# Two classical rows ahead of the Strassen chunks of a down projection, with its operand pieces loaded raw and split by ACT, DVE and POOL

## The chip, the cores and the metric

The kernel runs on one core of a Trainium2 chip. The metric is device time in microseconds (us) for one execution, and less is better. The profile is of one execution. Engines are named as there: PE (TensorE), DVE (VectorE), ACT (ScalarE), POOL (GpSimd) and SP (SyncE, which here only issues DMA).

## The reference

One step of a streaming encoder layer over T = 1072 tokens (16 meta, 1024 prompt, 32 decode), model width 1024. A mixing block (convolution heads and attention heads) comes first. The change is in the feed-forward behind it:

```python
h = rmsnorm(x, g)
u = h @ w_up                       # 1024 -> 2 x 2816
gate, up = u[..., :D_FF], u[..., D_FF:]
y = silu(depthwise_causal_conv(concat(gate_past, gate), dw_w, dw_b)) * up
return x + y @ w_down              # 2816 -> 1024, then the final rmsnorm
```

## The kernel before

Everything is fp32 carried as two parts: `hi` (an ACT cast) and `lo` (raw minus hi, on DVE), both made by `hilo`. A product takes three matmuls (hi hi, hi lo, lo hi). The 2816 hidden channels are 22 rows f = 0..21 of 128, and the 1024 outputs are 8 blocks m.

**Up projection.** Rows 0 and 1 are plain matmuls. Rows 2..21 use Strassen's scheme on 2x2 blocks: seven products q, each for two token halves p, 12 matmuls of 264 to 266 columns each (`product`, L1208), so 168 matmuls per f. The weight combinations of the next f are made by `w_forms` on ACT and DVE meanwhile; `gate_done` and `y_done` make row f of y. For f = 2..17 `y_done` stores the seven right-hand operands to DRAM (`yq`, and for q = 1 and 5 already split, `yh`). The rows 0, 1 and 18..21 are stored whole (`yd`).

**Down projection.** Rows 2..17 form two chunks c = 0, 1 of eight rows. For each chunk there are four Strassen steps mp = 0..3 (two output blocks each), 168 matmuls a step, over 14 operand pieces (q, p) of 128 x 1056 values. They live in the tiles `bh`, `bl` (q = 1..4) and `th`, `tl` (q = 5..7), where the up projection's own operands were. A piece can only be written when PE has finished its last product from the old content: `f_load` is called behind each product of f = 21 (for c = 0) and of step c = 0, mp = 3 (for c = 1). Ten of the 14 pieces come raw through a stage (`early`: row tiles and `rbt`; `late`: `rbt`, `rbg`, shown in the trace as `rb` and `rbg`), four come split from `yh` by POOL's queue. Results go from PSUM to the residual tiles `X` (`x` in the trace), by ACT copies or DVE adds. In c = 0 the old residual `xd` is added by POOL's accumulating DMAs behind each step. The six rows 0, 1, 18..21 stay classical: 18 matmuls for each of 8 blocks m in the end loop over `ENDS` (400, 400 and 256 columns), which also does the final norm (`final`).

PE's order is the order of the code (`manual_schedule`). In the end loop ACT's and DVE's orders are the code's too; elsewhere a scheduler orders them, and each engine then runs its list in order, waits included. PSUM tiles `mm` come from a pool of six.

Of the kernel before, what the change touches and what calls it, by code (L numbers as in the profile page):

```python
# [17 lines left out]
P = 128  # L18
# [74 lines left out]
DN = 264  # L93
FORD = (*range(2, 10, 2), *range(3, 10, 2), *range(10, 18, 2), *range(11, 18, 2), 0, 1, 18, 19, 20, 21)
# [62 lines left out]
def body(nc, tc, cp, wp, xp, dp, io):  # L157
# [922 lines left out]
    yh = dp.tile([2, P, 2, 2, 2, 4, DN], F32, tag="yh", name="yh")  # L1080
# [49 lines left out]
    with tc.tile_pool(name="psB", bufs=1, space=PSUM, reuse_waits="tile") as pf:  # L1130
# [5 lines left out]
        raws3 = [xf[1][:, i * 1024:i * 1024 + 1024] for i in range(3)]  # L1136
# [27 lines left out]
        def w_forms(key, src, raws):  # L1164
            w = ups[key] = Up()
            g, u, s = raws
            A, B = slice(0, 512), slice(512, 1024)
            nc.sync.dma_start(g, src[0])
            nc.sync.dma_start(u, src[1])
            yield  # L1170
            hg, lg, h12, l12, h34, l34, a22 = (free.pop(0) for _ in range(7))
            tt_ = nc.vector.tensor_tensor
            nc.scalar.copy(hg, g)
            tt_(out=s[:, A], in0=u[:, A], in1=u[:, B], op=ALU.add)
            tt_(out=s[:, B], in0=s[:, A], in1=g[:, A], op=ALU.subtract)
# [12 lines left out]
            used = (h12, l12, hg, lg, h34, l34, a22)
            free.extend(z for z in used if key != ("d", 0, 0) or not any(z is r for r in rawr))
# [77 lines left out]
        def y_done(f):  # L1267
# [38 lines left out]
        SEQ_ = (1, 5, 6, 2, 7, 3, 4)  # L1306
        FIRST, COPY = (1, 5, 2), (1, 5, 6, 4)
# [17 lines left out]
        def strassen(key, steps, dst, ns, fresh=True):  # L1325
            banks = {}
            for q, p in steps:
# [3 lines left out]
                product(banks[k], q, p, key, ns[p], q in FIRST)  # L1331
                for lo_, hi_, z in dst(*OUT[q], p):
                    if fresh and q in COPY:
# [75 lines left out]
        def rows(z, n):  # L1409
            z = z.rearrange("p a b c -> p (a b c)") if len(z.shape) == 4 else flat(z) if len(z.shape) == 3 else z  # L1410
            w = T - H0 if n == KD else ny
            return [z[:, i * w:i * w + ny] for i in range(n)]

        trow = [(h, l) for p in range(2) for h, l in zip(rows(THI[p], 3), rows(TLO[p], 3))]
        yrow = [trow[i] for i in (0, 3, 1, 4, 2, 5)]
        yf = (0, 1, 18, 19, 20, 21)
        early = [rows1[0][:, 0:ny], rows1[1][:, 0:ny], rbt[:, 0:ny]]
        early += early[:1] + 3 * early[1:]
        late = [rbt[:, 0:ny], rbg[:, 0:ny]]
        nst = [-1]  # L1420

        def stage(st):
            nst[0] += 1
            return st[nst[0] % len(st)]

        def f_load(c, q, p):
            if q in (1, 5):
                for j, z in enumerate(form(q, p, DN)):
                    nc.gpsimd.dma_start(z, yh[c, :, q // 5, j, p].bitcast(F32R))
                return  # L1430
            raw = stage(late if c else early)
            nc.sync.dma_start(raw, yq[c, :, q - 1, p].rearrange("p a b -> p (a b)"))
            hilo(*form(q, p, DN), raw.rearrange("p (a b) -> p a b", b=DN))

        def y_load(i):
            raw = stage(late)
            nc.sync.dma_start(raw, yd[yf[i]][:, NMETA:T])
            hilo(*yrow[i], raw)

        bhf, blf = flat(BH), flat(BL)  # L1440
# [9 lines left out]
        def d_src(m, f0, f1):  # L1450
            return d.wdn[m, :, f0:f1, :].rearrange("p a b -> p (a b)")

        def d_load(m):
            w = 6 * P
            if m < 4:
                hi, lo = free.pop(0), free.pop(0)
            else:
                hi, lo = (z[:, (m - 4) * 1024:(m - 4) * 1024 + 1024] for z in (bhf, blf))
            raw = fraw()
            nc.sync.dma_start(raw[:, :w], d_src(m, 16, 22))  # L1460
            hilo(hi[:, :w], lo[:, :w], raw[:, :w])
            return kv(hi[:, :w]), kv(lo[:, :w])

        def d_mm(ps, w, t0, n):
            at = t0 - NMETA
            mm3(ps, range(6), lambda k: w[0][:, k, :], lambda k: w[1][:, k, :],
                lambda k: yrow[k][0][:, at:at + n], lambda k: yrow[k][1][:, at:at + n])

        pairs = [(q, p) for q in SEQ_ for p in range(2)]
        apart = [(q, p) for p in (1, 0) for q in SEQ_]  # L1470

        def dn_forms(c, mp):
            if (c, mp) == (0, 0):
# [15 lines left out]

        for f in range(2, NF - 1):  # L1490
            run(up_strassen(f, pairs), w_forms(f + 1, [up_src(f + 1, u) for u in range(2)], raws3))
        run(up_strassen(NF - 1, apart), dn_forms(0, 0), lambda q, p: f_load(0, q, p),
            (1, 3, 5, 9, 10, 11, 12))
        ends = {}

        def last_hook(q, p):
            if p:
                if q in (5, 6, 7):
                    y_load(2 * (q - 5))
                    y_load(2 * (q - 5) + 1)  # L1500
                if q in (6, 2, 3, 4):
                    m = len(ends)
                    ends[m] = d_load(m)

        steps = [(c, mp) for c in range(2) for mp in range(4)]
        for i, (c, mp) in enumerate(steps):
# [153 lines left out]
```

## Time and profile before

| | |
|---|---|
| median of 3 runs | 1095.97 us (1094.5 to 1096.67) |
| the profiled execution | 1095.29 us |
| its span | 1093.5 us (1.79 us around it) |
| PE / DVE / ACT / POOL busy share | 96% / 79% / 46% / 15% |
| mean granted clock of PE | 0.988 |

PE is busy in nearly every slice, so time is lost where PE waits. Stages: mixing to about 352 us, up projection to about 825, down steps to 1009, end loop to 1082, final norm and stores to 1093.5.

### The profile page before, as it was taken

How to read it: one execution, taken by the hardware profiler on the slowest of the kernel's cores; microseconds unless marked ns; L12 is line 12 of the kernel's file. 1: busy time of each engine (PE TensorE's matmuls, PEld its weight loads, DVE VectorE, ACT ScalarE, POOL GpSimd, SP SyncE). 2: the span in 40 equal slices, each digit the busy share in tenths (PEclk: the TensorE clock that was granted, in tenths of full speed). 3: DMA queues.
4: the chain of work that ended last, by engine and by line, in shares of the span. 5: the costliest groups of instructions: out<-in, count | busy, mean ns of one | idle time of the engine just before them, and what ended most of it. 6: DMA issues, size and time to landing. Idle time of an engine off the chain costs nothing.

```text
span 1093.5 us, 19782 instructions
## 1 busy us (share of the span) xinstructions
PE 1050.1 (96%) x7741; PEld 1019.4 (93%) x7741; DVE 860.3 (79%) x1559; ACT 499.8 (46%) x1077; POOL 168.2 (15%) x205
## 2 busy tenths in 40 slices
PE   8999999989999989999999999999998999799996
PEld 7999997758999989999999999999997999799996
DVE  7799999999887797888888879888768447666344
ACT  8532227996766854344344344334335334213321
POOL 1111000012334010010110011010021131000232
PEclk9999998999999999999999999999999999899998
DMA  7344331125853111432432432332287469414113
GB/s 263 80 108 100 82 95 40 39 59 82 158 147 134 41 59 59 139 107 89 122 124 89 127 119 89 112 134 89 85 261 226 127 132 330 143 39 152 45 49 112
DMA packets 73062, 125.46 MB, mean 115 GB/s; under 512 B 11264, under 2 KB 53496, under 8 KB 72968
## 3 DMA queue, kind: packets, MB, share of 16 engines
q1 hardware_dynamic: 56232, 97.44, 27.4%
q0 software_dynamic: 16448, 26.54, 12.8%
q8 instruction: 61, 1.00, 0.4%
q14 instruction: 33, 0.27, 0.1%
q10 hardware_dynamic: 288, 0.22, 0.1%
HBM read 83.23 MB, written 31.83 MB: 105 GB/s over the span
## 4 chain that ended last, share of the span: by engine, by line
PE 55%; DVE 6%; DMA 3%; ACT 3%; issue 2%; POOL 0%; POOLq 0%; DVEq 0%; ACTq 0%; SPq 0%
PE mm L1208 46%; PE mm L241 3%; PE mm L239 3%; PE mm L240 3%; DMA x<-yq 1%; DVE tl L1146 1%; DMA raw<-wdn 1%; DVE bl L1146 1%; ACT hraw L1228 1%; DMA x<-wdn 0%; ACT th L1145 0%; DMA rbg<-yq 0%; DVE x L1336 0%; DVE sl L1146 0%; DMA rb<-yq 0%
## 5 line engine op out<-in xcount | busy, mean ns | idle before, releaser
L365 DVE SCALAR_TENSOR_TENSOR acc<-glu,prm,acc 128x1090 f32<-128x1090 f32 (+3 forms) x180 | 168.0, 968 | 0.4
L1208 PE MATMUL mm<-bh,sl 128*128 128x264 f32 (+1 forms) x752 | 163.0, 286 | 1.8 <-ACT bh L1145 1.3
L1208 PE MATMUL mm<-th,sl 128*128 128x264 f32 (+1 forms) x592 | 144.6, 287 | 2.6 <-ACT gx L1334 1.9
L1208 PEld LDWEIGHTS mm<-bh,sl 128*128 128x128 f32 x752 | 125.9, 190 | 2.3 <-ACT bh L1145 1.6
L1208 PE MATMUL mm<-bl,sl 128*128 128x264 f32 (+1 forms) x376 | 108.2, 288 | 0.9 <-DVE bl L1146 0.9
L1208 PEld LDWEIGHTS mm<-th,sl 128*128 128x128 f32 x592 | 104.1, 189 | 3.4 <-ACT gx L1334 2.1
L239 PE MATMUL mm<-hi,whi 128*128 128x352 f32 (+3 forms) x312 | 104.7, 336 | 0.7 <-ACT hi L274 0.7
L1208 PE MATMUL mm<-bh,whi 128*128 128x264 f32 (+1 forms) x384 | 102.2, 288 | 2.2 <-DVE x L1336 1.2
L240 PE MATMUL mm<-lo,whi 128*128 128x352 f32 (+3 forms) x312 | 102.3, 328 | 1.7 <-DVE lo L275 1.7
L1208 PE MATMUL mm<-bh,wlo 128*128 128x264 f32 (+1 forms) x384 | 101.6, 287 | 0.2 <-DVE x L1336 0.2
L241 PE MATMUL mm<-hi,wlo 128*128 128x352 f32 (+3 forms) x312 | 101.8, 326 | 0.0
L1208 PE MATMUL mm<-tl,sl 128*128 128x264 f32 (+1 forms) x296 | 85.1, 288 | 3.3 <-DVE tl L1146 3.2
L1336 DVE TENSOR_TENSOR x<-x,mm 128x264 f32<-128x264 f32 (+6 forms) x190 | 61.3, 352 | 31.8 <-PE mm L1208 31.1
L1334 ACT COPY x<-mm 128x264 f32<-128x264 f32 (+4 forms) x138 | 43.9, 339 | 80.1 <-PE mm L1208 75.4
L1208 PE MATMUL mm<-th,wlo 128*128 128x264 f32 (+1 forms) x272 | 77.7, 285 | 0.0
L1208 PE MATMUL mm<-th,whi 128*128 128x264 f32 (+1 forms) x272 | 77.6, 285 | 0.0
L1208 PEld LDWEIGHTS mm<-bh,whi 128*128 128x128 f32 x384 | 70.9, 192 | 2.8 <-ACT bh L1145 1.4
L1208 PEld LDWEIGHTS mm<-bl,sl 128*128 128x128 f32 x376 | 71.7, 191 | 1.1 <-DVE bl L1146 1.1
L1208 PEld LDWEIGHTS mm<-bh,wlo 128*128 128x128 f32 x384 | 70.6, 191 | 0.4 <-DVE x L1336 0.4
L240 PEld LDWEIGHTS mm<-lo,whi 128*128 128x128 f32 x312 | 59.2, 190 | 3.4 <-DVE lo L275 3.1
L1208 PE MATMUL mm<-bh,rawr 128*128 128x264 f32 (+1 forms) x272 | 61.5, 286 | 0.0
L239 PEld LDWEIGHTS mm<-hi,whi 128*128 128x128 f32 x312 | 59.1, 189 | 2.2 <-ACT hi L274 1.2
(387 smaller groups left out, 3099.7 us busy)
## 6 DMA issues: line engine op xcount, KB each, us to landing
x<-wup SPq DMA_DIRECT2D x40, 512.0 KB, 4.9
wlo<-raw POOLq DMA_DIRECT2D x16, 512.0 KB, 4.5
yh<-x SPq DMA_DIRECT2D x24, 264.0 KB, 4.9
yq<-x SPq DMA_DIRECT2D x24, 264.0 KB, 2.7
raw<-win SPq DMA_DIRECT2D x12, 512.0 KB, 3.4
raw<-wdn SPq DMA_DIRECT2D x12, 512.0 KB, 4.2
rb<-yq SPq DMA_DIRECT2D x9, 528.0 KB, 4.5
yq<-gx SPq DMA_DIRECT2D x16, 264.0 KB, 5.0
```

Source lines behind the costliest of these rows:

```text
L239: nc.tensor.matmul(ps, whi(k), xhi(k), start=first and i == 0, stop=False)
L240: nc.tensor.matmul(ps, whi(k), xlo(k), start=False, stop=False)
L241: nc.tensor.matmul(ps, wlo(k), xhi(k), start=False, stop=last and i == n - 1)
L365: nc.vector.scalar_tensor_tensor(out=a, in0=e[:, a0 + k:a1 + k], scalar=pcol("cw", p * CW + k), in1=a, op0=ALU.mult, op1=ALU.add)
L1146: nc.vector.tensor_tensor(out=lo, in0=raw, in1=hi.bitcast(F32), op=ALU.subtract)
L1208: nc.tensor.matmul(ps, w[:, j, :], x[:, j, :], start=first and j + i == 0, stop=j == 3 and i == 2, skip_group_check=True)
L1228: nc.scalar.activation(h[:, 2 * i * n + lo_:2 * i * n + hi_], src, AF.Copy, scale=pcol("g2", k))
L1334: nc.scalar.copy(z, banks[k][:, lo_:hi_])
L1336: nc.vector.tensor_tensor(out=z, in0=z, in1=banks[k][:, lo_:hi_], op=ALU.add)
```

## The change

In words:
1. `yh` is gone. All 14 pieces of a chunk are loaded raw from `yq` through a queue of stages (`Feed`: `fill` starts a DMA when a stage is free, `take` splits the piece and gives the stage back). In the fourth Strassen step, behind whose products chunk 1's pieces are loaded, there are three stages (`late`: `rbt`, `gx0`, `rbg`) in place of two. Ten of the 28 low parts are subtracted on POOL.
2. Rows 0 and 1 move from the end loop to a place between f = 21 and the first Strassen step: 24 classical groups of six matmuls (384, 352 and 320 columns), written to `X` by ACT. Chunk 0's pieces are split among them. The end loop has four rows, 12 matmuls per block.
3. All Strassen results are now added by DVE (`fresh=False`), and `xd` is added after steps 0 and 1, as twelve DMAs of POOL's queue.
4. f = 21 runs its products in the order 1, 6, 7, 5, 3, 2, 4, both halves of a product together, instead of all of p = 1 before p = 0. The steps run mp = 3, 2, 1, 0.
5. `w_forms` takes its second weight in two halves of 512 and needs one stage less; `gx0` is free of it.
6. In f = 0 and 1, two steps of the operand preparation `t1s` and the `gate_done(0)` move by a group or two.

```diff
-FORD = (*range(2, 10, 2), *range(3, 10, 2), *range(10, 18, 2), *range(11, 18, 2), 0, 1, 18, 19, 20, 21)
+FORD = (0, 1, *range(2, 10, 2), *range(3, 10, 2), *range(10, 18, 2), *range(11, 18, 2), 18, 19, 20, 21)
...
-        def hilo(hi, lo, raw):
+        def hilo(hi, lo, raw, eng=None):
             nc.scalar.copy(hi, raw)
-            nc.vector.tensor_tensor(out=lo, in0=raw, in1=hi.bitcast(F32), op=ALU.subtract)
+            return (eng or nc.vector).tensor_tensor(out=lo, in0=raw, in1=hi.bitcast(F32), op=ALU.subtract)
...
-            g, u, s = raws
+            g, a, b = raws
...
-            nc.sync.dma_start(g, src[0])
-            nc.sync.dma_start(u, src[1])
+            for z, y in ((g, src[0]), (a, src[1][:, A]), (b, src[1][:, B])):
+                nc.sync.dma_start(z, y)
...
-                for j, z, hi, lo in ((0, b11, form_row(G), form_row(G, 2 * DN)), (1, t1, form_row(Tm, 2 * DN), b11)):
-                    hilo(hi.bitcast(F32R), lo.bitcast(F32R), z)
-                    nc.sync.dma_start(yh[c, :, j, 0, :, i, :], hi)
-                    nc.sync.dma_start(yh[c, :, j, 1, :, i, :], lo)
+                put(1, b11)
+                put(5, t1)
...
-            if i == 2:
+            if i == 1:
                 next(last_rms)
                 gate_done(0)
-            next(t1s)
+            if i % 2:
+                next(t1s)
...
+            def fill(self):
+                while self.jobs and self.stages:
+                    dst, src, view = self.jobs.pop(0)
+                    z = self.stages.pop(0)
+                    raw = view(z)
+                    nc.sync.dma_start(raw, src)
+                    self.ready.append((dst, raw, z))
+
+            def take(self, eng=None, keep=True):
+                dst, raw, z = self.ready.pop(0)
+                self.last = hilo(*dst, raw, eng).ins
+                if keep:
+                    self.stages.append(z)
+                self.fill()
...
-        run(up_strassen(NF - 1, apart), dn_forms(0, 0), lambda q, p: f_load(0, q, p),
-            (1, 3, 5, 9, 10, 11, 12))
+        run(up_strassen(NF - 1, [(q, p) for q in SEQL for p in range(2)]), None, first_hook)
+        TAKES = {0: (None, None), 1: (nc.gpsimd,), 3: (nc.gpsimd,), 4: (None,), 9: (nc.gpsimd,), 12: (None,), 14: (nc.gpsimd,), 17: (None,), 18: (nc.gpsimd,)}
+        for i, (m, b) in enumerate([(m, b) for m in range(KD - 1, -1, -1) for b in (1, 2)] +
+                                   [(m, 0) for m in range(KD - 1, -1, -1)]):
+            for e in TAKES.get(i, ()):
+                feed.take(e, i >= 9)
+                if i == 3:
+                    feed.stages += late
+                    feed.fill()
+            t0, n = YB[b]
+            ps = mmt()[:, :n]
+            d_mm(ps, [z[:, m % 4] for z in wa[m // 4]], arow, t0, n)
+            nc.scalar.copy(X[b][:, m, t0 - OB[b][0]:], ps)
...
-            if mp == 3:
-                hook = last_hook if c else lambda q, p: f_load(1, q, p)
+            if i == 3:
+                feed = Feed([f_job(1, q, p) for q, p in pairs], late)
+                hook = lambda q, p: feed.take(nc.gpsimd if (q, p) in GQ else None)
...
-            run(strassen(("d", c, mp), pairs if i else apart, dn_dst(mp), (DN, DN), c == 0),
-                dn_forms(*steps[i + 1]) if i < 7 else None, hook,
-                *(() if i else ((1, 3, 5, 9, 12, 12, 13),)))
-            if c == 0:
-                for b, (t0, n) in enumerate(YB):
-                    nc.gpsimd.dma_start(X[b][:, 2 * mp:2 * mp + 2, t0 - OB[b][0]:], xd[:, 2 * mp:2 * mp + 2, t0 - H0:t0 - H0 + n],
-                                        accum_op=ALU.add)
+            run(strassen(("d", c, mp), pairs, dn_dst(mp), (DN, DN), False),
+                dn_forms(*STEPS[i + 1]) if i < 7 else None, hook)
+            for z in {0: (0, 1), 1: (3, 2)}.get(i, ()):
+                xd_add(z)
```

How the lists of three engines change. First POOL, at the fourth Strassen step (`bl`, `bh`, `tl`, `th` are operand tiles, `rb` is the stage `rbt`). Before, POOL only issues DMAs there:

```order
L1429 DMA bh_3096<-yh_3103 128x4x264
L1429 DMA tl0_3620<-yh_3103 128x4x264
L1429 DMA th0_3618<-yh_3103 128x4x264
L1429 DMA tl1_3621<-yh_3103 128x1056
L1429 DMA th1_3619<-yh_3103 128x1056
L1515 DMA x0_2250<-xd_3100 128x2x320
L1515 DMA x1_2251<-xd_3100 128x2x384
L1515 DMA x2_2252<-xd_3100 128x2x352
```

After, POOL subtracts four low parts of chunk 1, behind the last adds of `xd`:

```order
L1538 DMA x1_2251<-xd_3100 128x2x384
L1538 DMA x2_2252<-xd_3100 128x2x352
L1145 TENSOR_TENSOR tl1_3620<-rb_75,th1_3618 128x1056
L1145 TENSOR_TENSOR bl_3097<-rb_75,bh_3096 128x4x264
L1145 TENSOR_TENSOR tl1_3620<-rb_75,th1_3618 128x1056
L1145 TENSOR_TENSOR bl_3097<-rb_75,bh_3096 128x4x264
```

All four come through the same stage `rbt`, and no DMA of `yh` is left on that queue.

Second ACT, behind f = 21 (L1335 and L1527 evict PSUM tiles `mm`; L1144 casts a raw stage). Before, at the start of the down steps:

```order
L1145 CAST bh_3096<-x2_2252 128x4x264
L1145 CAST th1_3619<-rb_75 128x1056
L1334 COPY x0_2250<-mm_8608 128x266
L1145 CAST bh_3096<-x2_2252 128x4x264
L1334 COPY x1_2251<-mm_8740 128x176
L1334 COPY x2_2252<-mm_8740 128x88
```

After, at the start of the classical groups:

```order
L1144 CAST th0_3617<-rb_75 128x4x264
L1144 CAST th1_3618<-x1_2251 128x1056
L1335 COPY x0_2250<-mm_8500 128x266
L1335 COPY x0_2250<-mm_8514 128x264
L1144 CAST whi_3635<-raw_8617 128x512
L1527 COPY x1_2251<-mm_8726 128x384
L1144 CAST bh_3096<-x1_2251 128x4x264
L1527 COPY x2_2252<-mm_8736 128x352
L1144 CAST sl_4085<-raw_8617 128x512
L1527 COPY x1_2251<-mm_8748 128x384
L1144 CAST th1_3618<-rb_75 128x1056
L1527 COPY x2_2252<-mm_8761 128x352
```

In both lists casts of staged pieces stand between evictions; after, the evictions are those of classical groups (`mm_8726` is the first), one PSUM tile each.

Third DVE, in the step behind the fourth (L1337 adds a product to `X`, L1145 subtracts a low part, L1176, L1177 and L1182 are weight combinations). After:

```order
L1176 TENSOR_TENSOR raw_9886<-raw_9886 128x512
L1337 TENSOR_TENSOR x2_2252<-x2_2252,mm_9901 128x264
L1145 TENSOR_TENSOR bl_3097<-rbg_3098,bh_3096 128x4x264
L1177 TENSOR_TENSOR raw_9886<-raw_9885,raw_9886 128x512
L1337 TENSOR_TENSOR x0_2250<-x0_2250,mm_9981 128x264
L1145 TENSOR_TENSOR sl_4085<-raw_9885,whi_3635 128x1024
L1145 TENSOR_TENSOR sl_4085<-raw_9886,wlo_3638 128x512
L1337 TENSOR_TENSOR x1_2251<-x1_2251,mm_9995 128x176
L1337 TENSOR_TENSOR x2_2252<-x2_2252,mm_9995 128x88
L1145 TENSOR_TENSOR bl_3097<-gx0_3621,bh_3096 128x4x264
L1337 TENSOR_TENSOR x0_2250<-x0_2250,mm_9887 128x56
```

The adds of products stand behind subtractions of pieces, and the last piece of chunk 1 on DVE (`gx0`) comes well inside the step that uses it.

## Rows read from the trace of the kernel before

**Rows 1.** The head of the page: the span, and each engine's busy time with its share of the span and its count of instructions.

```profile
span 1093.5 us, 19782 instructions
...
PE 1050.1 (96%) x7741; PEld 1019.4 (93%) x7741; DVE 860.3 (79%) x1559; ACT 499.8 (46%) x1077; POOL 168.2 (15%) x205
```

**Rows 2.** Busy time by stretch. Columns: the stretch (us), its length, then for PE, its weight loads, DVE, ACT and POOL the busy us and (x instructions); the granted clock of PE; the busy share of the DMA engines; GB/s.

```profile
400.00:500.00 100.00, 100.00 (x817) 100.00 (x817) 84.24 (x118) 41.50 (x80) 8.70 (x14) 1.00 0.28 94
808.30:853.00 44.70, 35.25 (x254) 32.97 (x253) 32.82 (x44) 21.11 (x35) 7.25 (x9) 0.96 0.84 256
870.00:900.00 30.00, 30.00 (x248) 30.00 (x247) 13.07 (x24) 10.55 (x27) 9.87 (x11) 1.00 0.58 130
925.00:946.00 21.00, 14.22 (x80) 12.76 (x79) 15.05 (x23) 8.01 (x9) 0.00 (x0) 0.84 0.64 175
```

**Rows 3.** What PE waited for between 805 and 855 us: its line, the instruction that let it go, us in total, times, longest.

```profile
PE mm L1208 <- DVE bl L1146: 2.0, 3, 0.9
PE mm L1208 <- ACT gx L1334: 1.9, 1, 1.9
PE mm L1208 <- DVE tl L1146: 1.9, 1, 1.9
PE mm L1208 <- DVE x L1336: 1.4, 2, 1.2
```

**Rows 4.** The same between 922 and 948 us.

```profile
PE mm L1208 <- DVE tl L1146: 3.2, 1, 3.2
PE mm L1208 <- DVE bl L1146: 2.2, 2, 1.2
PE mm L1208 <- ACT bh L1145: 1.3, 1, 1.3
```

**Rows 5.** DMA issues between 895 and 950 us: transfer, queue, count, size, median us from issue to landing.

```profile
rb<-yq SPq DMA_DIRECT2D x4, 528.0 KB, 5.4
rbg<-yq SPq DMA_DIRECT2D x4, 528.0 KB, 4.8
...
bl<-yh POOLq DMA_DIRECT2D x2, 528.0 KB, 9.5
```

**Rows 6.** The same between 800 and 855 us.

```profile
x<-yq SPq DMA_DIRECT2D x6, 528.0 KB, 6.8
rb<-yq SPq DMA_DIRECT2D x5, 528.0 KB, 3.6
```

**Rows 7.** ACT between 800 and 1000 us by line and shape: busy us, mean ns of one, idle before.

```profile
L1145 ACT CAST th<-rb 128x1056 fp32r<-128x1056 f32 x7 | 7.5, 1078 | 5.8 <-PE mm L1208 2.2 <-DMA rb<-yq 2.1 <-DMA rb<-yd 1.4
L1334 ACT COPY x<-mm 128x264 f32<-128x264 f32 x18 | 6.8, 379 | 17.8 <-PE mm L1208 17.6
...
L1145 ACT CAST sl<-raw 128x512 fp32r<-128x512 f32 x7 | 4.4, 623 | 12.9 <-PE mm L1208 8.8 <-DVE raw L1176 3.2 <-DVE raw L1179 0.7
```

**Rows 8.** DVE between 800 and 1000 us, in the same columns.

```profile
L1336 DVE TENSOR_TENSOR x<-x,mm 128x264 f32<-128x264 f32 x38 | 16.0, 424 | 6.2 <-PE mm L1208 5.6 <-issue 0.6
L1146 DVE TENSOR_TENSOR tl<-rb,th 128x1056 fp32r<-128x1056 f32 x7 | 8.8, 1254 | 1.6 <-ACT th L1145 1.6
...
L1176 DVE TENSOR_TENSOR raw<-raw 128x512 f32<-128x512 f32 x6 | 4.1, 684 | 0.0
```

**Rows 9.** POOL over the whole span, in the same columns.

```profile
L1556 POOL TENSOR_TENSOR rb<-rb,gx 128x400 f32<-128x400 f32 x7 | 7.4, 1054 | 16.2 <-ACT gx L1554 16.2
...
L1556 POOL TENSOR_TENSOR rb<-rb,gx 128x256 f32<-128x256 f32 x3 | 2.2, 740 | 6.6 <-ACT gx L1554 6.6
```

**Rows 10.** Four timeline answers set one under the other: start, us, engine and instruction. POOL and then DVE at 1043 us, the same DVE instruction at 1070 us, and DVE and POOL at 350 us.

```profile
1043.58 1.05 POOL L1556 TENSOR_TENSOR rb<-rb,rbg 128x400 f32<-128x400 f32 x1
...
1043.63 1.02 DVE L255 SCALAR_TENSOR_TENSOR stat<-stat 128x4 f32<-128x4 f32 x1 [1.15 <-POOL stat L254]
...
1070.14 0.16 DVE L255 SCALAR_TENSOR_TENSOR stat<-stat 128x4 f32<-128x4 f32 x1 [1.81 <-POOL stat L254]
...
350.39 1.23 DVE L1146 TENSOR_TENSOR wlo<-raw,whi 128x1024 fp32r<-128x1024 f32 x1 [1.13 <-ACT whi L1145]
...
350.90 1.38 POOL L271 TENSOR_TENSOR rb<-rb,acc 128x352 f32<-128x352 f32 x1 [2.58 <-ACT acc L270]
```

**Rows 11.** What PE waited for between 381 and 392 us.

```profile
PE mm L241 <- DVE wlo L1146: 2.1, 1, 2.1
PE mm L239 <- ACT whi L1145: 1.7, 1, 1.7
```

**Rows 12.** Timeline of the last round of the end loop: two PE rows, the ACT row between them, and DVE.

```profile
1067.18 0.95 PE L252 MATMUL R<-ones,rb 128*128 128x1 f32 x8
...
1072.32 1.05 PE L263 MATMUL R<-diag,ones 128*128 128x128 f32 x8
...
1071.44 1.27 ACT L260 ACTIVATE diag<-ident,stat 128x128 f32<-128x128 f32 x4
...
1079.84 0.42 DVE L1553 TENSOR_TENSOR x<-x,mm 128x256 f32<-128x256 f32 x1 [0.38 <-PE mm L241]
...
1081.97 0.42 DVE L1553 TENSOR_TENSOR x<-x,mm 128x256 f32<-128x256 f32 x1 [0.38 <-PE mm L241]
1082.31 1.42 DVE L1530 SCALAR_TENSOR_TENSOR x<-x,prm,R 128x48 f32<-128x48 f32 x4
1083.82 0.16 DVE L253 TENSOR_SCALAR stat<-R 128x2 f32<-128x2 f32 x1
```

More of the change, by code (lines that the diff above doesn't have):

```diff
@@ L1331, in strassen @@
                 product(banks[k], q, p, key, ns[p], q in FIRST)
+                copy = fresh and (OUT[q], p) not in begun
+                begun.add((OUT[q], p))
                 for lo_, hi_, z in dst(*OUT[q], p):
-                    if fresh and q in COPY:
+                    if copy:
                         nc.scalar.copy(z, banks[k][:, lo_:hi_])
@@ L1341, in up_strassen @@
             for q, p in strassen(f, steps, up_dst(f), PNS):
-                if (q, p) == (3, 1) and f < NF - 1:
+                if (q, p) == (3 if f < NF - 1 else 2, 1):
                     gate_done(f)
                 yield q, p
-            if f == NF - 1:
-                gate_done(f)
             y_done(f)
@@ L1388, in body @@
             group(1, u, p, c)
+            if i in (0, 2):
+                next(t1s)
             if i == 3:
@@ L1407, in body @@
         ny = T - NMETA
[L1409 to L1440, printed above, removed]
+        def row(q, p):
+            a = (q - 5) * 4 * PNS[p]
+            return [flat(z[p].rearrange("p a b c -> p (a b) c"))[:, a:a + ny] for z in (THI, TLO)]
+        arow = row(7, 0), row(7, 1)
+        crow = row(5, 0), row(5, 1), row(6, 0), row(6, 1)
+        late = [rbt[:, 0:ny], gx0[:, 0:ny], rbg[:, 0:ny]]
@@ new lines, in body, with __init__ @@
+        class Feed:
+            def __init__(self, jobs, stages):
+                self.jobs, self.stages, self.ready = list(jobs), list(stages), []
+                self.fill()
[11 more added lines that the diff above has]
+                    self.stages.append(z)
+                self.fill()
@@ L1488, in run @@
                 pass
+        GQ = ((5, 1), (2, 0), (7, 1), (4, 0))
+        STEPS = [(c, mp) for c in range(2) for mp in (3, 2, 1, 0)]
         for f in range(2, NF - 1):
-            run(up_strassen(f, pairs), w_forms(f + 1, [up_src(f + 1, u) for u in range(2)], raws3))
-        run(up_strassen(NF - 1, apart), dn_forms(0, 0), lambda q, p: f_load(0, q, p),
-            (1, 3, 5, 9, 10, 11, 12))
-        ends = {}
-        def last_hook(q, p):
[L1497 to L1503, printed above, removed]
@@ L1505, in body @@
[L1505 to L1516 removed]
+            run(up_strassen(f, pairs), w_forms(f + 1, up_srcs(f + 1), raws))
@@ new lines, in body, with first_hook @@
+        first = []
+        def first_hook(q, p):
+            if q == 7:
+                if p == 0:
+                    feeda.take(keep=False)
+                    feeda.jobs.append(w_job(wa[0], 0, 4, 0, 2))
+                    feeda.stages.append(x1a)
+                    feeda.ready.append(feeda.ready.pop(0))
+                    feeda.fill()
+                else:
+                    feeda.take(keep=False)
+                    feeda.take(keep=False)
+            if q == 5 and p:
+                first.append(dn_forms(*STEPS[0]))
+                next(first[0])
+            if q == 3:
+                if p:
+                    feeda.take(keep=False)
+                    feed.stages += [x1b, x2b, rbt]
+                    feed.fill()
+            if q == 2 and p:
+                feeda.take(keep=False)
+                feed.stages += [x1a, x2a]
+                feed.fill()
@@ new lines, in body, with xd_add @@
+        feed = Feed([f_job(0, q, p) for q in (7, 3) for p in range(2)], late)
+        for e in (None, None, None, nc.gpsimd):
+            feed.take(e)
+        mark = feed.last
+        def xd_add(mp):
+            with tc.issue_after(mark):
+                for b, (t0, n) in enumerate(YB):
+                    nc.gpsimd.dma_start(X[b][:, 2 * mp:2 * mp + 2, t0 - OB[b][0]:],
+                                        xd[:, 2 * mp:2 * mp + 2, t0 - H0:t0 - H0 + n], accum_op=ALU.add)
+        wend = []
@@ L1544, in body @@
             for m in range(KD):
-                if not pos and m + 4 < KD:
-                    ends[m + 4] = d_load(m + 4)
                 ps = mmt()[:, :n]
-                d_mm(ps, ends[m], t0, n)
+                d_mm(ps, [z[:, m % 2] for z in wend[m // 2]], crow, t0, n)
                 if m == 0:
```

102 lines of the change are left out of this document (58 added, 44 removed).

## The prediction

> **What bounds the kernel now.** I read the head of the page, the table of stretches, PE's waits in the stretches where PE falls behind, and the DMA landings there. PE is busy 1050.1 of 1093.5 us, DVE 860 [rows 1], so PE sets the time wherever it has its operands. Its own pace is read in the up projection: 817 matmuls in 100 us with nothing missing, 0.1224 us each, 1.47 us for a product of twelve [rows 2]. The count of matmuls in a stretch then tells what PE lost in it, waits and half clock together:
> - **T1**, the change from the up projection to the down steps: 44.70 us held 254 matmuls, worth 254 x 0.1224 = 31.1, so 13.6 us were lost, at a mean granted clock of 0.96 [rows 2].
> - **T2**, the change to chunk 1: 21.00 us held 80, worth 9.8, so 11.2 us were lost, clock 0.84 [rows 2].
>
> Between them PE loses nothing (30.00 of 30.00). A few records can be missing, so each loss may be some tenths smaller. In T1 PE waits for the low and high parts of the new pieces, once 1.9 us for an eviction (`gx`), and for DVE adds [rows 3]; in T2 only for parts of pieces [rows 4]. The reason is the turn of a stage: landing 4.8 to 5.4 us [rows 5], cast 1.08 [rows 7], subtraction 1.25 [rows 8], about 7.3 us. Two stages give a piece per 3.6 us; a product wants one per 1.47. So 24.8 us is all that the change can win at T1 and T2.
>
> **The change, part by part.** I count from the first matmul of a stage, at 1.47 us a product, in the order of the lists.
>
> *T1.* f = 21 takes 14 x 1.47 = 20.6 us. The classical groups do work that the end loop loses, so they cost PE nothing in sum; by the column (18 matmuls of 256 columns take 1081.97 - 1079.84 = 2.13 us, [rows 12]) they take 1.07, 0.98 and 0.89 us for 384, 352 and 320 columns, 23.5 together. In that time chunk 0's pieces can come, and Strassen starts at 44.1. What can still stop PE is ACT's list, where casts that wait for a DMA stand ahead of evictions, with six PSUM tiles as cover (about 6 us). The longest chain is the stage `rbt`: cast of piece (6,0) from 19.1 (behind the first weights' casts), POOL's subtraction, landing of (5,1), cast, POOL, landing of (4,0), cast. A subtraction of 1056 columns on POOL isn't in the trace; 400 columns take 1.054 and 256 take 0.740 [rows 9], 2.18 ns a column, so I estimate 2.48. Sum: 19.1 + 1.08 + 2.48 + 4.8 + 1.08 + 2.48 + 4.8 + 1.08 = 36.9. Behind it the eviction of group 10 (0.4) ends at 37.3, and group 16, which wants that tile, could start at 20.6 + 8 x 2.05 = 37.0. So 0.3 lost there. Two other margins are thin: the low part of the second weight tile of rows 0 and 1 (ready near 20.3, wanted at 20.8), and pieces (7,1) and (3,1), about 2 us ahead of their use. Bounds: 0 with landings of 3.6, about 6 with 6.8 [rows 6]. I take **2.0**, since 4.8 lies nearer the first.
>
> *T2.* Fourth step, t = 0 at its start. Three stages are full, and the pieces are needed from 20.6 on. Stage `rbt` again is the slow one, since POOL empties it four times: its first piece is split by DVE at 5.9 (the next weights land near 2.5, 4.8 behind an issue at -2.3; two casts 0.62 and 1.08 [rows 7], two adds, the subtraction 1.25), then four turns of 4.8 + 1.08 + 2.48 = 8.36 bring the low part of (4,0) at 39.3. PE wants it 26 products in, at 38.2: 1.1 lost. DVE is the second limit. In two steps it has 28 adds (half of them whole, 0.424; half in two parts, about 0.57), 13.9; twenty weight instructions (eighteen of 512 columns at 0.684, two of 1024, about twice that), 15.0; ten subtractions, 12.5 [rows 8]: 41.4 busy, but an instruction starts about 0.08 before the last one ends (1082.31 against 1081.97 + 0.42, [rows 12]), so some 35.6 of the 41.2 us. It fits, but adds wait behind subtractions that wait for casts that wait for DMA: by my count the adds of (7,0) and (7,1) in the fourth step and of (6,0) and (7,0) in the fifth come between 0.7 us early and 1 us late. I take **2.5** in all. Bounds: 0 with 3.6, 5 with 5.4, 10 with 6.8 a landing.
>
> *End loop.* Its groups shrink by a third. In the last 256-column round two groups lie between PE's sums (L252, 1067.18) and its spread of the factor (L263, 1072.32), which needs ACT's four `diag` tiles (1071.44 to 1072.71) [rows 12]. With groups of 1.42 PE is there 1.42 earlier and that chain isn't: 0.9 lost. Then DVE has an add and four scalings per group, 0.34 + 1.42 = 1.76 (or 1.7 with overlap), where PE now takes 1.42; over the last groups it falls behind by 0.9, and the last sums wait for the last add. Before, DVE waited for PE there. Together **+1.8**, bounds 0 and 4.
>
> *T0.* Rows 0 and 1: PE waits 1.7 and 2.1 us for the split of a weight tile [rows 11]. Two preparation steps leave the lists ahead of that split. The second wait stays if its subtraction stays where it is; **-1.0**, bounds 0 and -3.
>
> *At nothing.* `w_forms` has one DVE instruction more for the same columns, and even rows lose two splits: DVE is 84% busy in the up projection and PE 100% [rows 2]. If that cover were gone, 0.684 for each of 20 rows would be 14 us. The adds that move from ACT to DVE, eight a step, put 8 x 0.42 to 0.57 = 4 us on a DVE that was busy 13.07 of 30 us [rows 2]. The `xd` DMAs are first read two steps after their issue; even a POOL transfer of 9.5 us [rows 5] is hidden by 20.6.
>
> **Sum**, against the profiled execution's 1095.3, 0.7 under the median: 1095.3 - 24.8 + 2.0 + 2.5 + 1.8 - 1.0 = 1075.8, so **1076**.
>
> **The rivals.**
>
> *Landings stay long.* The `rbt` chain has two landings in T1 and four in T2. At 6.8 us, T1's median before, each adds 2.0: +12, **1088**. For it: T1 moves some 14 pieces in 40 us now as then. Against: most of the 256 GB/s of T1 [rows 2] went with POOL's split loads, which are gone; `rb` landed in 3.6.
>
> *POOL and DVE get in each other's way.* A DVE instruction of 128x4 that takes 0.16 us took 1.02 while POOL subtracted for 1.05; elsewhere DVE took its 1.23 for 1024 columns while POOL stretched to 1.38 for 352 [rows 10]. So one can hold up the other. If each of POOL's four subtractions at T2 holds DVE for its whole 2.48, DVE has 35.6 + 9.9 = 45.5 of 41.2 us, 4.3 too much; and where DVE goes first, POOL's chain grows by up to 4 x 1.25 = 5. That is +9: **1085**. The Trainium skill says this (SBUF — State Buffer, "SBUF: two separate sides"): GpSimd and a DVE instruction with two SBUF inputs take one pair of ports as an exclusive lock for a whole instruction. The 1.02 agrees; by that rule the sum would be the 1085 just given. Adds read PSUM on one side and would escape it, and four such meetings must each fall on a thin margin, so I hold it less likely.
>
> *Slower than before.* ACT and DVE run their lists in order, so a late landing stops evictions and adds that have nothing to do with the piece. The place is `rbt`'s chain: six landings, 4.5 us lost already at 4.8. The gain of 24.0 (24.8 + 1.0 - 1.8) is gone when 6 e + 4.5 = 24.0, at e = 3.3, that is from 8.1 us a landing. POOL's loads took 9.5 [rows 5]; at that, 6 x 4.7 = 28 more, **1104**. Against: SP's own loads of the same size took 4.8 to 6.8 in the same crowd.
>
> *It doesn't do what it says.* The new weight order makes each of the 20 rows of the up projection a microsecond longer, DVE's 84% being the average over 20 us of which the first part may be full. That is +20: **1096**. Against: PE had no idle there at that load [rows 2], and the work per row doesn't grow.
>
> **How the numbers follow.** Forecast 0.58 (own range 1070 to 1081), long landings 0.19, ports 0.11, slower 0.09, no change 0.03. Under 0.2% (2.2 us) a measurement of this kernel can't be told from no change. The first three are faster: 0.88. The range starts at 1067 (all three remaining losses at nothing and T0 at 3: 1095.3 - 24.8 - 3 = 1067.5) and reaches to 1090, past the long landings; outside lie the last two cases and little else.
>
> **What would show it.** In the new profile: T1 and T2 with over 95% of the matmuls that the pace gives, no half clock there; POOL's 128x1056 subtraction near 2.5 us; SP's `yq` landings near 4.8; waits of PE, if any, at (4,0) of the fifth step and at the third quarter of the classical groups; PE waiting about 0.9 us at L263 in the last round. I am wrong if POOL's subtractions take much longer, if adds (`x`) become PE's main wait in steps four and five, or if the up projection has fewer than 817 in 100 us.

## The result and the profile after

The changed kernel takes 1083.85 us (median; 1083.37 to 1084.88), the kernel before 1095.24 us beside it: ratio 0.9899, 95% interval 0.988 to 0.9919. It is faster by 11.4 us where 19.3 were forecast (1095.3 to 1076). The profiled execution took 1084.88 us, 1.8 of it outside the span.

The head of the page after, against [rows 1]: PE is busy 3 us less, DVE 14 us more.

```profile
span 1083.1 us, 19942 instructions
...
PE 1046.9 (97%) x7741; PEld 1016.4 (94%) x7741; DVE 874.4 (81%) x1616; ACT 499.5 (46%) x1072; POOL 180.7 (17%) x199
```

Busy time by stretch, in the columns of [rows 2]: the up projection, the classical groups, two stretches of the first two Strassen steps, and T2.

```profile
400.00:500.00 100.00, 100.00 (x817) 100.00 (x816) 83.88 (x123) 41.05 (x82) 11.34 (x14) 1.00 0.27 86
...
820.80:850.00 29.20, 25.05 (x147) 23.03 (x146) 24.16 (x23) 18.58 (x36) 12.76 (x7) 1.00 0.57 186
...
850.00:875.70 25.70, 25.70 (x212) 25.70 (x211) 17.35 (x34) 9.38 (x13) 15.85 (x11) 1.00 0.83 215
...
870.00:900.00 30.00, 30.00 (x247) 29.89 (x246) 18.22 (x46) 5.31 (x8) 7.64 (x7) 1.00 0.96 192
921.90:957.00 35.10, 31.77 (x256) 31.19 (x255) 32.48 (x57) 18.07 (x21) 10.71 (x4) 1.00 0.75 232
```

The up projection keeps its 817 matmuls, and the half clock of T1 and T2 is gone (0.96 and 0.84 before, 1.00 now). But the classical groups, 23.5 us of work, take 29.2: 5.7 lost. In T2, 256 matmuls are worth 256 x 0.1224 = 31.3 of 35.1 us: 3.8 lost. What PE waited for, in the columns of [rows 3]: first between 820 and 850 us, then between 921 and 957.

```profile
PE mm L239 <- ACT x L1527: 4.0, 5, 1.2
```

```profile
PE mm L1209 <- DVE x L1337: 3.1, 2, 2.1
PE mm L1209 <- ACT th L1144: 0.2, 1, 0.2
```

PE hardly waits for a piece any more (0.2 us for `th`), as it did in [rows 3, 4]. It waits for PSUM tiles: in the classical groups for ACT's evictions, in T2 for DVE's adds. The timeline shows what stood ahead of these. POOL's subtractions, four of the ten (start, us):

```profile
823.02 2.92 POOL L1145 TENSOR_TENSOR tl<-x,th 128x1056 fp32r<-128x1056 f32 x1
...
829.76 3.36 POOL L1145 TENSOR_TENSOR tl<-rb,th 128x1056 fp32r<-128x1056 f32 x1 [0.49 <-ACT th L1144]
...
923.80 2.86 POOL L1145 TENSOR_TENSOR tl<-rb,th 128x1056 fp32r<-128x1056 f32 x1 [29.35 <-ACT th L1144]
933.08 2.48 POOL L1145 TENSOR_TENSOR bl<-rb,bh 128x1056 fp32r<-128x1056 f32 x1 [6.42 <-ACT bh L1144]
```

DVE beside them:

```profile
823.52 3.54 DVE L1256 TENSOR_TENSOR gx<-gx,rbg 128x1060 f32<-128x1060 f32 x1
...
830.70 3.53 DVE L1262 SCALAR_TENSOR_TENSOR x<-gx,prm,x 128x1058 f32<-128x1058 f32 x1
...
835.97 1.30 DVE L1262 SCALAR_TENSOR_TENSOR x<-gx,prm,x 128x1058 f32<-128x1058 f32 x1
...
924.91 2.83 DVE L1145 TENSOR_TENSOR sl<-raw,wlo 128x1024 fp32r<-128x1024 f32 x1
...
934.22 2.46 DVE L1145 TENSOR_TENSOR bl<-gx,bh 128x1056 fp32r<-128x1056 f32 x1 [0.44 <-ACT bh L1144]
```

The same L1262 takes 1.30 us with POOL idle and 3.53 with POOL subtracting. Each of the four long rows ends 1.1 us behind the end of a POOL row (823.52 + 3.54 = 827.06 against 823.02 + 2.92 = 825.94, and so on): it has waited for POOL and then done its own 1.2 to 1.3 us. ACT, in the classical groups:

```profile
835.47 0.62 ACT L1144 CAST sl<-raw 128x512 fp32r<-128x512 f32 x1 [2.95 <-DVE raw L1185]
...
837.30 1.09 ACT L1265 ACTIVATE x<-x 128x1058 f32<-128x1058 f32 x1 [0.84 <-DVE x L1262]
...
848.48 1.75 ACT L1527 COPY x<-mm 128x320 f32<-128x320 f32 x5 [1.57 <-DMA yd<-x]
```

So DVE's stretched gate chain of row 21 (L1256, L1262) delays a weight combination (L1185), and ACT's cast of it and the evictions behind that cast come late; then ACT's silu (L1265), and at the end the store of that row (`yd`), which the last evictions overwrite. PE waits behind each of these. The next load of the stage `rbg` and the store were issued at 839.7 and 842.3 us; in the first kernel of experiment 4, where this chain isn't stretched, they were issued at 835.3 and 837.2.

### The profile page after: what moved, and what is told of

Its sections match the earlier page's. It is cut to its first block, busy times and chain, and to the rows that moved or that the text cites. A ratio compares the mean times of both kernels' runs of the same rounds, so it can differ in the third digit from the quotient of the medians.

```text
span 1083.1 us, 19942 instructions
## 1 busy us (share of the span) xinstructions
PE 1046.9 (97%) x7741; PEld 1016.4 (94%) x7741; DVE 874.4 (81%) x1616; ACT 499.5 (46%) x1072; POOL 180.7 (17%) x199
## 4 chain that ended last, share of the span: by engine, by line
PE 55%; DVE 6%; DMA 3%; ACT 3%; issue 2%; POOL 1%; POOLq 0%; DVEq 0%; SPq 0%; ACTq 0%
PE mm L1209 49%; PE mm L241 2%; PE mm L239 2%; PE mm L240 2%; DMA raw<-wdn 1%; DVE bl L1145 1%; DMA gx<-yq 1%; DVE tl L1145 1%; DVE x L1262 1%; ACT hraw L1229 1%; DVE sl L1145 1%; DMA yd<-x 1%; DVE x L1582 1%; DVE gx L1256 0%; DVE wlo L1145 0%
## 5 line engine op out<-in xcount | busy, mean ns | idle before, releaser
L1209 PE MATMUL mm<-bh,sl 128*128 128x264 f32 (+1 forms) x912 | 214.7, 285 | 1.0 <-DVE x L1337 1.0
L1209 PEld LDWEIGHTS mm<-bh,sl 128*128 128x128 f32 x912 | 157.6, 189 | 1.2 <-DVE x L1337 1.2
L1209 PE MATMUL mm<-th,rawr 128*128 128x266 f32 (+1 forms) x640 | 121.3, 285 | 0.0
L1337 DVE TENSOR_TENSOR x<-x,mm 128x264 f32<-128x264 f32 (+7 forms) x238 | 75.8, 346 | 47.9 <-PE mm L1209 47.8
L1209 PEld LDWEIGHTS mm<-th,rawr 128*128 128x128 f32 x640 | 101.2, 189 | 0.0
L1209 PE MATMUL mm<-th,sl 128*128 128x264 f32 (+1 forms) x352 | 93.1, 285 | 0.2 <-ACT th L1144 0.2
L1209 PE MATMUL mm<-tl,rawr 128*128 128x266 f32 (+1 forms) x320 | 91.4, 286 | 0.0
L1209 PE MATMUL mm<-bl,whi 128*128 128x264 f32 (+1 forms) x272 | 77.4, 285 | 0.0
L1144 ACT CAST sl<-x 128x512 fp32r<-128x512 f32 (+1 forms) x41 | 29.7, 726 | 76.0 <-PE mm L1209 40.8
L1209 PEld LDWEIGHTS mm<-th,sl 128*128 128x128 f32 x352 | 64.2, 189 | 0.5 <-ACT th L1144 0.4
```

What stands on the lines that cost most here:

```text
L1209: nc.tensor.matmul(ps, w[:, j, :], x[:, j, :], start=first and j + i == 0, stop=j == 3 and i == 2, skip_group_check=True)
L1337: nc.vector.tensor_tensor(out=z, in0=z, in1=banks[k][:, lo_:hi_], op=ALU.add)
```

## The experiments

**1. Extra subtractions on POOL, in the sixth Strassen step**, where the kernel after loses nothing. Their results are read by nobody.

```diff
+            elif i == 5:
+                def hook(q, p):
+                    if q in (5, 2, 3):
+                        nc.gpsimd.tensor_tensor(out=late[1], in0=late[0], in1=late[2], op=ALU.subtract)
```

> The changed kernel with six more POOL subtractions of 128x1056 (their result is not used) during the sixth Strassen step, where POOL has nothing to do. Lock theory: each takes 2.4 to 3.4 us, DVE's weight combinations there (two SBUF inputs, 0.68 us each) take up to 2.5 us when they meet one, its adds from PSUM keep 0.42. Rival (no contention, the long DVE instructions of the changed kernel came from something else): 0.68 and 0.42 throughout.

Measured: 1091.34 us in its one execution, 6.5 above the profiled execution of the kernel after. POOL in that step, and DVE beside it:

```profile
952.13 16.70 POOL L1564 TENSOR_TENSOR gx<-rb,rbg 128x1056 f32<-128x1056 f32 x6 [3.33 <-DVE bl L1145]
```

```profile
952.38 2.74 DVE L1182 TENSOR_TENSOR raw<-raw 128x512 f32<-128x512 f32 x1
955.04 0.42 DVE L1337 TENSOR_TENSOR x<-x,mm 128x264 f32<-128x264 f32 x1
955.38 2.60 DVE L1145 TENSOR_TENSOR wlo<-raw,sl 128x512 fp32r<-128x512 f32 x1
...
958.31 2.54 DVE L1185 TENSOR_TENSOR raw<-raw 128x512 f32<-128x512 f32 x1
960.77 2.92 DVE L1145 TENSOR_TENSOR sl<-raw,wlo 128x512 fp32r<-128x512 f32 x1
...
964.29 2.25 DVE L1145 TENSOR_TENSOR wlo<-raw,sl 128x512 fp32r<-128x512 f32 x1
```

One of POOL's subtractions takes 16.70 / 6 = 2.78 us. A DVE instruction of 512 columns with both inputs in SBUF takes 2.25 to 2.92 instead of 0.68 [rows 8]: five such rows beside six of POOL's. The add in their midst, with one input in PSUM, keeps its 0.42. The first half of the step, in this kernel and then the same half in the kernel after (columns of [rows 2]):

```profile
957.10:973.90 16.80, 13.35 (x87) 12.85 (x86) 13.71 (x20) 2.55 (x4) 11.42 (x5) 0.80 0.45 143
```

```profile
954.70:971.50 16.80, 16.80 (x140) 16.80 (x139) 12.84 (x33) 3.77 (x6) 0.00 (x0) 1.00 0.30 91
```

53 matmuls fewer are 53 x 0.1224 = 6.5 us. PE waits there for DVE's adds alone (3.5 us in two waits); beside these waits the granted clock fell to a mean of 0.80. So the blocking is shown by itself. The Trainium skill (SBUF — State Buffer, "SBUF: two separate sides") gives GpSimd and a DVE instruction with two SBUF inputs one pair of ports under an exclusive lock for a whole instruction. The 2.25 to 2.92 beside 2.78, and the 0.42 of the add, agree with it.

**2. Chunk 1 without POOL.** `GQ = ()`: the four subtractions of T2 go to DVE, chunk 0 keeps its six on POOL.

> Only the four GpSimd subtractions of the second chunk (in step 4) go back to VectorE; the first chunk keeps its own on GpSimd. Theory (a GpSimd subtraction stretches every VectorE instruction with two SBUF inputs that runs beside it): step 4 loses 0.4 us instead of 4.2, as in the kernel without any GpSimd subtraction, and nothing else moves: 1083.85 - 3.8 = 1080 us. Rival (step 4 loses because its pieces land late): it loses about 4 us as before, and the time stays at 1084.

Measured: 1082.03 us (1081.5 to 1082.15), ratio 0.988 (0.9857 to 0.9904). T2, shifted with its step:

```profile
922.10:957.20 35.10, 34.73 (x279) 34.07 (x278) 34.16 (x66) 18.03 (x21) 0.00 (x0) 1.00 0.73 232
```

279 matmuls where the kernel after has 256: 1.0 us lost instead of 3.8, with four more subtractions on DVE. The profiled execution gained 2.8 (1084.88 to 1082.07), 1.8 is the difference of the medians; the two ranges of times part, the intervals of the ratios overlap. So POOL's help at T2 cost 2 to 3 us in this pair.

**3. No POOL at all; and POOL only for chunk 1.** In the first, all low parts go to DVE. In the second, `GQ` stays and only chunk 0's go to DVE.

```diff
-        GQ = ((5, 1), (2, 0), (7, 1), (4, 0))
+        GQ = ()
...
-        for e in (None, None, None, nc.gpsimd):
+        for e in (None, None, None, None):
```

> The changed kernel with all 28 low parts subtracted on DVE, none on POOL. Theory (a POOL subtraction locks DVE out of its own two-input subtractions, so it gives DVE no relief): the long DVE instructions of the changed kernel (2.43, 3.54, 3.53, 2.33 us around 821 to 855 us, 2.83, 2.46, 2.55 around 925 to 950) go back to 0.68 to 1.3 us, the classical groups lose under 3 us in place of 5.6, and the time is the changed kernel's or up to 4 us less: 1080 to 1084. Rival (POOL carries a load that DVE has no room for): DVE, with ten subtractions of 1.25 us more, falls behind at both changes, and the time is 1087 or more. Rival (long landings alone are the cause): the stalls stay where they are, 1083 to 1085, and the waits for DMA in front of ACT's casts are as long as now.

> The changed kernel with POOL's six subtractions for chunk 0 on DVE, the four for chunk 1 still on POOL. Lock theory: the losses at the classical groups fall from 5.6 to under 3 us (three long DVE instructions there cost 6.2 us, six subtractions on DVE cost 7.5 but spread over 40 us), those of steps four and five stay at 4.2; 1080 to 1083. If POOL's help is needed for chunk 0: 1086 or more.

Measured: 1085.34 us (1084.23 to 1085.61) and 1090.0 us (1088.53 to 1090.64). The first, in the classical groups and in the stretch behind them:

```profile
819.10:842.30 23.20, 23.20 (x146) 23.20 (x146) 19.27 (x23) 16.28 (x31) 11.46 (x7) 1.00 0.68 186
842.30:868.40 26.10, 17.88 (x127) 16.95 (x126) 16.67 (x29) 11.20 (x16) 2.35 (x2) 0.87 0.88 241
```

The classical groups lose nothing (23.2 us), so their 5.7 came from POOL. The kernel with POOL for chunk 1 alone doesn't lose in the groups either, but 9.9 us behind them (145 matmuls in 27.6 us) and 3.9 at T2 (262 in 36.0). The two kernels differ only in the four subtractions at T2 and lie 4.7 us apart: more than the 1.8 of experiment 2.

But in both the first Strassen step then loses much: in the first kernel 26.1 - 127 x 0.1224 = 10.6, where the kernel after lost nothing. PE waited there mostly for evictions (842 to 872 us, first kernel):

```profile
PE mm L1209 <- ACT x L1527: 6.0, 2, 3.2
PE mm L1209 <- DVE tl L1145: 2.1, 1, 2.1
```

I first read this as DVE being late with chunk 0's pieces. The DMA issues between 831 and 850 us say otherwise (columns of [rows 5]); first without POOL, then the kernel after:

```profile
rbg<-yq SPq DMA_DIRECT2D x2, 528.0 KB, 8.9
x<-xd POOLq DMA_DIRECT2D x2, 384.0 KB, 9.7
...
raw<-wdn SPq DMA_DIRECT2D x2, 256.0 KB, 11.3
```

```profile
rbg<-yq SPq DMA_DIRECT2D x2, 528.0 KB, 5.8
...
raw<-wdn SPq DMA_DIRECT2D x2, 256.0 KB, 5.0
```

The `xd` adds were held back by an order behind `mark`, chunk 0's last subtraction. With the subtraction on DVE that order no longer held, and POOL issued the first of them at 831 us, 32 us earlier. The evictions for which PE waits stand in ACT's list behind casts of `rbg` and `raw` and behind the store of row 21, which landed late. These two kernels therefore change two things at once, and the next two part them.

**4. Only the last subtraction of chunk 0 on POOL**, so that the `xd` adds stay behind it, and **the kernel after with the `xd` adds loose**. The first edit is against the first kernel of experiment 3, the second against the kernel after.

```diff
-        for e in (None, None, None, None):
+        for e in (None, None, None, nc.gpsimd):
```

```diff
-            with tc.issue_after(mark):
+            if True:
```

> As the kernel after, but of all GpSimd subtractions only the last one of the first chunk is left there, the one behind which the twelve accumulating DMAs of xd are queued; all others on VectorE. The kernel without any of them had lost that order: its xd DMAs were issued from 831 us on, instead of 863, and its yq, wdn and yd DMAs of 835 to 848 us landed 9 to 15 us after their issue, instead of 5 to 7. Theory (two causes in that kernel: no stretching, but the bus full of xd): here the middle groups take 23 us instead of 29.1, the first Strassen step behind them loses at most 2 us, step 4 loses 0.4 instead of 4.2: 1083.85 - 6 + 1 - 3.8 = 1075 us. Rival (VectorE with all the subtractions is itself too late for the first step): the step loses about 10 us as in the kernel without any, and the time is 1085 us.

> As the kernel after, GpSimd's subtractions included, but the xd DMAs are no longer ordered behind the first chunk's last subtraction; they still stand behind GpSimd's other work that the order puts ahead of them. Theory (early xd transfers delay the first chunk's pieces): the yq and yd landings between 835 and 850 us get longer than the 5 to 7 us of the kernel after, and the first Strassen step behind the middle groups loses several us more, up to 10: 1086 to 1094 us. If the order holds even without the edge, nothing moves: 1084 us. Rival (landings do not depend on xd): landings as before, time 1084 us with the xd DMAs issued early.

Measured: 1076.79 us (1074.75 to 1077.17), ratio 0.9827 (0.9798 to 0.9857), and 1089.48 us (1086.83 to 1091.82), ratio 0.9951 (0.9933 to 0.9969). The first, in the classical groups and T2:

```profile
819.30:843.60 24.30, 23.46 (x146) 23.18 (x146) 20.09 (x23) 17.61 (x34) 6.70 (x3) 1.00 0.66 214
915.50:949.40 33.90, 31.81 (x255) 31.06 (x254) 31.83 (x61) 17.23 (x20) 0.00 (x0) 1.00 0.75 238
```

24.3 us for the groups, and the first Strassen step has no wait. With nine subtractions moved from POOL to the busier DVE the kernel is 7.1 us faster by the medians: what was short was not DVE's time for its own instructions. The second, behind the classical groups:

```profile
847.50:874.30 26.80, 22.73 (x171) 22.11 (x170) 17.66 (x29) 10.14 (x15) 8.19 (x6) 0.94 0.90 237
```

171 matmuls are worth 20.9 of 26.8: 5.9 lost, 5.6 in the medians, because six of the twelve transfers were issued from 839 us on instead of 863. So the late pieces of experiment 3 were the doing of `xd`, and not of DVE. Which load is late differs: here SP's loads of 256 KB landed in 5.1 us, not 11.3, and PE waited for parts of pieces (3.0 us) more than for evictions (1.1).

**5. Two stages in the fourth step instead of three**, on the kernel with one POOL subtraction: `Feed(..., late[::2])`.

> As the kernel with one GpSimd subtraction (1076.8 us), but step 4 loads its operand pieces through two stages (rbt, rbg) instead of three, as the kernel before did. Theory (with two stages a piece waits for its predecessor's subtraction and then 4 to 5 us for its own landing, which the third stage hides): step 4 loses 8 to 13 us instead of 3.2, near the 11.2 of before: 1082 to 1087 us. Rival (the gain in step 4 comes from the operand pieces that are no longer stored and loaded as high and low parts, and the third stage is worth nothing): it loses 3 to 4 us, 1077 us.

Measured: 1086.34 us (1085.5 to 1087.07), 9.5 more. T2, and what PE waited for between 905 and 955 us:

```profile
916.80:969.20 52.40, 45.90 (x339) 44.12 (x338) 40.73 (x78) 21.65 (x25) 0.00 (x0) 0.93 0.56 175
```

```profile
PE mm L1209 <- DVE bl L1145: 3.3, 4, 0.9
PE mm L1209 <- ACT bh L1144: 1.8, 2, 1.4
PE mm L1209 <- DVE tl L1145: 1.2, 1, 1.2
```

52.4 - 339 x 0.1224 = 10.9 lost, with the half clock, and the waits are again for pieces, as in [rows 4]. The third stage alone brings nearly all that the change wins at T2 (11.2 lost before).

**6. The gate of row 0 back behind the third group** (`if i == 2`), and apart from it **the diagonal of the end loop made earlier**: in `final`, two `next(rms)` and then two `yield` in place of one after the other.

> The changed kernel with gate_done(0) and the last norm step back at the third of the second four groups of f = 0, as in the kernel before; the steps of t1s stay where the change put them. Theory (the moved gate_done puts four DVE instructions, 4.7 us, ahead of the low part of the weight tile that PE waits 3.2 us for, and PE runs 6.8 us at half clock behind that wait): wait under 1.5 us, half clock gone or 3.4 us, 2 to 4 us less than the changed kernel: 1080 to 1082. Rival (the weights arrive late from DRAM, whatever DVE does): no change, 1083 to 1085.

> As the kernel after, but ScalarE makes the scaled diagonal of each end round one output row earlier, so that it stands ahead of the squares behind which it waits. Theory of the prediction (the wait of 0.8 us ahead of L263 in the second round comes from that queue): the gap at L263 in the middle of the end loop goes, the end loop takes 49.8 us instead of 50.6, 1083.1 us. Rival (the wait moves on, since VectorE is then late with the scaling in the same place): the end loop takes 50.6 us again, 1084 us.

Measured: 1084.07 us (1082.42 to 1084.86) and 1083.54 us (1082.52 to 1085.38), neither to be told from 1083.85. In the profiled executions something moved all the same. The weight split for which PE waits, after and with the gate moved back:

```profile
386.17 1.22 DVE L1145 TENSOR_TENSOR wlo<-raw,whi 128x1024 fp32r<-128x1024 f32 x1
```

```profile
385.07 1.22 DVE L1145 TENSOR_TENSOR wlo<-raw,whi 128x1024 fp32r<-128x1024 f32 x1
```

The split runs 1.1 earlier and the first Strassen matmul starts at 405.35 instead of 407.26; PE's wait for the split is 3.2 us in both, though under 1.5 was expected. T2 then lost 1.4 more. The wait at L263, again after and with the earlier diagonal (the final one of 2.1 is in both):

```profile
PE R L263 <- ACT diag L260: 2.9, 2, 2.1
```

```profile
PE R L263 <- ACT diag L260: 2.3, 2, 2.1
```

From the loop's start to its last sums it takes 50.9 us instead of 51.8.

**7. One POOL subtraction, the gate and the diagonal together.**

> As the kernel with one GpSimd subtraction (1076.8 us), with the row-0 gate where the kernel before had it (behind the third group) and with the earlier diagonal of the end rounds. Theory: first Strassen matmul at 405.3 us instead of 406.0, the wait at L263 0.8 us shorter: 1076.8 - 0.7 - 0.8 = 1075.3 us. Rival (both only move a wait): 1076.8 us.

Measured: 1074.47 us (1073.58 to 1075.75), ratio 0.9807 (0.9789 to 0.9826): the fastest kernel here, 9.4 us below the change as it was made. Against the 1076.79 of experiment 4 (1074.75 to 1077.17) the ranges overlap, and the two ran on different chips, so whether the two small edits give anything on top is not shown. The profiled execution began Strassen 1.7 us earlier (404.31) and lost that again: the classical groups took 27.0 us instead of 24.3, with POOL idle in both but for two copies. PE's waits of 800 to 846 us there, and ACT:

```profile
PE mm L239 <- ACT x L1527: 2.4, 1, 2.4
```

```profile
841.26 1.07 ACT L1144 CAST bh<-rbg 128x1056 fp32r<-128x1056 f32 x1 [4.45 <-DMA rbg<-yq]
```

PE waits there for the eviction behind this cast, which waits for a landing: the limit that the prediction had named for the groups. In experiment 4 the same cast came at 841.17 and PE, later by then, waited 0.8.

## Why the prediction was right, and where it was not

The direction and most of the mechanism held; the time is 8 us above the forecast, inside the range given. In us, by stage, from the profiled executions (after; and with one POOL subtraction):

| | forecast | after | one on POOL |
|---|---|---|---|
| T0 | -1.0 | +1.1 | -0.1 |
| left at T1 | 2.0 | 6.8 | 1.9 |
| left at T2 | 2.5 | 4.0 | 3.0 |
| end loop and tail | +1.8 | +2.5 | +2.3 |
| time | 1075.8 | 1084.9 | 1077.1 |

T0 is the start of the first Strassen matmul (406.13 before, 407.26, 405.99). T1 is the excess of the classical groups over 23.5, and 1.0 to 1.1 in the second half of f = 21. T2 is counted over the two steps from their first matmul, 336 x 0.1224 = 41.1 us without loss. The measured terms, put into the sum of the forecast, give 1084.9 and 1077.6.

- **The 24.8 us to be won** were there: T1 and T2 have full clock, and hardly a piece is late. Experiment 5 shows the turn of a stage to be the reason at T2, as argued. At T1 no run parts the classical groups from the new order of f = 21 and the raw loads; that the groups gave the pieces their time stays argued.
- **T1, 2.0, is the term that failed**: 6.8. The chain of `rbt` was not what cost. POOL's subtraction, estimated at 2.48, took 2.43 to 3.36, and the landings of `rb` had a median of 5.0 over the whole run. What was left out is that DVE stands still meanwhile. With one POOL subtraction left the term is 1.9, near the forecast. The six kernels with POOL in the groups lost 4.7 to 5.8 there; of the five without, four lost at most 1.0, and the one of experiment 7 lost 3.4, behind a landing.
- **T2, 2.5**: 4.0, in the place and by the adds named as the sign of error. Over all runs with three stages, the six kernels with POOL there lost 3.2 to 5.8, the four without 0.3 to 3.0.
- **The rival of the ports** was what happened, but in another place: it priced T2 at +9, where POOL cost 2 to 5, and did not look at T1, where it cost 5. That 1084 comes so near its 1085 is luck. It was held to 0.11 because "four such meetings must each fall on a thin margin". With ten subtractions of 2.7 us beside a DVE that is over 80% busy even with POOL idle (20.09 of 24.3 in the classical groups, 31.83 of 33.9 at T2, experiment 4), a meeting is nearly certain, and the thin margin was a queue: one stretched gate chain holds up ACT's evictions.
- **Long landings** came in part. Between 800 and 855 us `rb` landed in 6.4 in the kernel after, near this rival's 6.8; at T2 in 4.1. They don't explain the loss of the groups: in the first kernel of experiment 3 it was 6.3, and the groups lost nothing. One reason against the rival was misread: of T1's 11.5 MB before (808.3 to 853 us) POOL's queue moved 2.6, not most. Landings longer still, from loose `xd` adds, did cost (experiments 3 and 4). That `xd` is "hidden by 20.6" was true for its reader and not for the loads beside it; only the order behind `mark` kept them apart. The two rows of `rb`, after and without POOL:

```profile
rb<-yq SPq DMA_DIRECT2D x5, 528.0 KB, 6.4
```

```profile
rb<-yq SPq DMA_DIRECT2D x5, 528.0 KB, 6.3
```

- **T0** has the wrong sign. The two preparation steps did leave DVE's list ahead of the split, but the gate moved in ahead of it, with both L1262. PE's waits there are 3.5 us, 0.3 less than in [rows 11], but the granted clock between 384 and 400 us is 0.79 where it was 0.89. In the other runs with this placement the first Strassen matmul came between 405.9 and 407.0, so T0 is near 0 and the 1.1 partly chance; with the gate behind the third group it came at 405.35 and 404.31.
- **End loop**: the wait of 0.9 at L263 in the last round was 0.8, and experiment 6 took most of it away. Behind the last product of the loop the time grew by 1.2 (11.8 to 13.0), where 0.9 was given.
- **At nothing**: the up projection and DVE's extra adds cost nothing, as said ([rows 2]; 18.22 busy of 30 at 870 to 900).

Open: why the two steps of T2, with POOL idle there, lose 0.3 us (experiment 3, first kernel), 0.8 (experiment 7), 1.2 (experiment 2) or 3.0 (experiment 4). PE waits for adds, and some of these stand behind subtractions that wait for landings; but the median landings of experiments 4 and 7 are near each other (4.2 to 4.5 and 4.3 to 4.6 us), so they don't settle it.

## What to carry to other kernels

Before work is moved from a busy DVE to an idle POOL, look at what DVE does in that stretch: if it mostly combines two SBUF tiles, each of POOL's instructions can hold DVE for nearly its own length, and the move can lose even where DVE is the busier engine. A DMA that nobody waits for still needs a place: put it behind the loads that somebody waits for, and see that the order survives when the instruction that carries it changes engine. And when an experiment gives no gain, compare the DMA issues before blaming the engine that was given the work.

## What the hardware showed that was not expected

- The blocking may work both ways. Beside an unbroken run of DVE instructions POOL's copies of 128x2 took 2.92 and 3.17 us (experiment 4), and 0.58 and 0.66 in the kernel after; each of the four ended within 0.05 us of the end of a DVE instruction. No run tried this by itself.

```profile
822.28 2.92 POOL L1257 COPY stout<-gx 128x2 f32<-128x2 f32 x1 [24.50 <-DVE gx L1256]
825.14 3.17 POOL L1258 COPY stout<-gx 128x2 f32<-128x2 f32 x1
```

- Accumulating DMAs of 320 to 384 KB on POOL's queue landed 5 to 17 us after their issue. SP's loads of 256 KB beside them took 11.3 us instead of 5.0 in experiment 3, and 5.1 in experiment 4, where SP's loads went out a little ahead of them.
